# Rotated q-k scores on one core: blocks transposed in place, three input tiles each, q loads a step earlier, rotations in pairs

## Chip, cores, metric

One core of one Trainium2 chip (trn2). The metric is the device time of one execution in microseconds. The profiled span is about 1.7 us shorter than the same execution's time.

## The reference

```python
# batch 16, seq 512, heads 16, dim 64; q, k: [16, 512, 16, 64] fp32; cos, sin: [512, 32]
q_rot = concat([q1 * cos - q2 * sin, q1 * sin + q2 * cos])   # q1, q2: halves of dim
k_rot = the same of k
scores = einsum('bshd,bthd->bsht', q_rot, k_rot)             # [16, 512, 16, 512] fp32
```

67.24 MB come in, 268.44 MB go out.

## The kernel before

A step is one quarter of a batch (128 rows of s, all 16 heads); there are 64. Row s is p*4+c, so that each partition reads and writes long runs (packets of 16 and 32 KB in the trace). VectorE rotates q and k in place in the loaded tile (two products, one sum), TensorE transposes 128x128 blocks into PSUM, VectorE or ScalarE copies them to kT or qT, TensorE forms the scores (two heads at a time, 64 rows of the array each), ScalarE copies these to one of three staging tiles, and SyncE issues the store.

```python
    in_pool = ctx.enter_context(tc.tile_pool(name="in", bufs=2))
    kt_pool = ctx.enter_context(tc.tile_pool(name="kt", bufs=2))
    qt_pool = ctx.enter_context(tc.tile_pool(name="qt", bufs=2))
    stage_pool = ctx.enter_context(tc.tile_pool(name="stage", bufs=3))
    ...
        for i in range(C, NST):                 # C = 4, NST = 64
            tr = {}
            if i + 1 < NST:
                tr[1], tr[3] = ("q", i + 1, 0), ("q", i + 1, 1)
            if i + C < NST:
                tr[5], tr[6] = ("k", i + C, 0), ("k", i + C, 1)
            dve = []
            if i + 2 < NST:
                dve += rope("q", i + 2)
            if i + 1 + C < NST:
                dve += rope("k", i + 1 + C)
            ...
            for p in range(HP):                 # 8 pairs of heads
                scores(i, p, st)
                if p not in tr:
                    continue
                if tr[p][0] == "q":
                    run(dve[:1])
                    dve = dve[1:]
                    transposed(*tr[p], nc.vector.tensor_copy)
                else:
                    transposed(*tr[p], nc.scalar.copy)
            run(dve)
            if i % C == C - 2:
                load("q", i // C + 2)
            elif i % C == C - 1:
                load("k", i // C + 3)
```

The last store is cut: all but the last two heads first, then these as a piece of 116 rows and one of 12.

Of the kernel before, what the change touches and what calls it, by code (L numbers as in the profile page):

```python
# [10 lines left out]
def kernel(  # L11
# [8 lines left out]
    nc = tc.nc  # L20
    fp32 = mybir.dt.float32
# [3 lines left out]
    B, S, H, D = q.shape  # L25
    HD = D // 2
    P = 128
    C = S // P
    HP = H // 2
    NST = B * C  # L30
    G = H // C

# [3 lines left out]
    kt_pool = ctx.enter_context(tc.tile_pool(name="kt", bufs=2))  # L36
    qt_pool = ctx.enter_context(tc.tile_pool(name="qt", bufs=2))
# [9 lines left out]
    o_v = out.rearrange("b (p c) h t -> b c p h t", c=C)  # L47
# [5 lines left out]
    ss_v = ss_t.rearrange("p c x j -> p c (x j)")  # L53



    st_first = [stage_pool.tile([P, H, S], fp32, tag="stage", name="st") for _ in range(2)]
    early = stage_pool.tile([P, 2 * C * H * D], fp32, tag="stage", name="early")
# [12 lines left out]
    batches = {}  # L71

    def load(which, b):

        if b >= B:
            return
        t = in_pool.tile([P, C, H * D], fp32, tag=which + "_in", name=which + "_sb")
        batches[which, b] = t
        nc.sync.dma_start(t.rearrange("p c (h d) -> p c h d", h=H), dram[which][b])

    def rope(which, n):


        part = part_pool.tile([P, H * D], fp32, tag="part", name="part")
        if n < C:
            x = units[which, n]
            sv, k1, k2 = "p c (g j) -> p c g j", {"j": HD}, {"j": D}
            cs = cos_t.unsqueeze(2).to_broadcast((P, C, 2 * G, HD))
            ss = ss_v.unsqueeze(2).to_broadcast((P, C, G, D))
            pv = part.rearrange("p (c g j) -> p c g j", c=C, j=D)  # L90
            x5 = x.rearrange("p c (h x j) -> p c h x j", x=2, j=HD)
            p5 = part.rearrange("p (c h x j) -> p c h x j", c=C, x=2, j=HD)
            adds = [(x5[:, :, :, y], p5[:, :, :, 1 - y]) for y in range(2)]
        else:
            x = batches[which, n // C][:, n % C]
            sv, k1, k2 = "p (g j) -> p g j", {"j": HD}, {"j": D}
            cs = cos_t[:, n % C].unsqueeze(1).to_broadcast((P, 2 * H, HD))
            ss = ss_v[:, n % C].unsqueeze(1).to_broadcast((P, H, D))
            pv = part.rearrange(sv, **k2)
            x4 = x.rearrange("p (h x j) -> p h x j", x=2, j=HD)  # L100
            swapped = bass.AP(part.tensor, part.offset + HD, [part.ap[0], (D, H), (-HD, 2), (1, HD)])
            adds = [(x4, swapped)]
        xs, xc = x.rearrange(sv, **k2), x.rearrange(sv, **k1)

        def products():
            nc.vector.tensor_tensor(pv, xs, ss, op=mult)  # L106
            nc.vector.tensor_tensor(xc, xc, cs, op=mult)  # L107

        def sums():
            for y, z in adds:  # L110
                nc.vector.tensor_tensor(y, y, z, op=add)  # L111

        return [products, sums]

    kT = {}
    qT = {}

    def transposed(which, n, g, copy):


        bank = ps_t_pool.tile([P, 4, P], fp32, tag="ps_t", name="bank")
        for x in range(4):
            if n < C:
                src = units[which, n][:, x, P * g : P * (g + 1)]
            else:
                src = batches[which, n // C][:, n % C, P * (4 * g + x) : P * (4 * g + x + 1)]
            nc.tensor.transpose(bank[:, x, :], src, ident)  # L127
        src = bank
        if which == "q":
            if n not in qT:  # L130
                qT[n] = qt_pool.tile([P, HP, P], fp32, tag="qT", name="qT_t")
            dst = qT[n][:, 4 * g : 4 * g + 4, :]
        else:
            b = n // C
            if b not in kT:
                kT[b] = kt_pool.tile([P, HP, S], fp32, tag="kT", name="kT_t")
            if n < C:
                dst = kT[b][:, 2 * n + g].rearrange("p (t c) -> p t c", c=C)
                src = bank.rearrange("p c t -> p t c")
            else:  # L140
                dst = kT[b][:, 4 * g : 4 * g + 4, P * (n % C) : P * (n % C + 1)]
        copy(out=dst, in_=src)  # L142

    def store(i, st):
        o = o_v[i // C, i % C]
        if i < NST - 1:
            nc.sync.dma_start(o, st)
            return

        h = H - 2  # L150
        nc.sync.dma_start(o[:, :h], st[:, :h])
        nc.sync.dma_start(o[:116, h:], st[:116, h:])
        nc.sync.dma_start(o[116:, h:], st[116:, h:])

    def scores(i, p, st):

        ps = ps_s_pool.tile([P, 2, S], fp32, tag="ps_s", name="ps")
        b = i // C
        if b == 0:
            c, hp = divmod(p, 2)  # L160
            lhs, rhs = qT[i][:, C * hp + c], kT[0][:, 2 * i + hp]
        else:
            lhs, rhs = qT[i][:, p], kT[b][:, p]
        for r in range(2):
            po, rh = ps[:, r, :], rhs[64 * r : 64 * r + 64, :]
            nc.tensor.matmul(  # L166
                out=po, lhsT=lhs[64 * r : 64 * r + 64, :], rhs=rh, start=True, stop=True
            )
        so, si = st[:, 2 * p : 2 * p + 2, :], ps
        if b > 0:  # L170
            so = so.rearrange("s r (t c) -> s r t c", c=C)
            si = si.rearrange("s r (c t) -> s r t c", c=C)
        nc.scalar.copy(out=so, in_=si)  # L173
        if b == 0 and p % 2 == 1:
            c = p // 2
            nc.sync.dma_start(o_v[0, c, :, G * i : G * (i + 1)], st[:, G * c : G * (c + 1)])
        elif b > 0 and p == HP - 1:
            store(i, st)
# [9 lines left out]
    with tc.manual_schedule():  # L188
# [6 lines left out]
        load("q", 1)  # L195
# [8 lines left out]
        for i in range(C):  # L204
            st = st_first[i] if i < 2 else stage_pool.tile([P, H, S], fp32, tag="stage", name="st")
# [6 lines left out]
            for p in range(HP):  # L212
                scores(i, p, st)
                if p in (0, 1) and i > 0:
                    run(dve[:1])
                    dve = dve[1:]
                    transposed("k", C + i - 1, p, nc.vector.tensor_copy)
                if p == 3 and i < 2:
                    load("kq"[i], 2)
# [9 lines left out]
        for i in range(C, NST):  # L229
            tr = {}  # L230
# [5 lines left out]
            if i + 2 < NST:  # L236
                dve += rope("q", i + 2)
            if i + 1 + C < NST:
                dve += rope("k", i + 1 + C)
            st = stage_pool.tile([P, H, S], fp32, tag="stage", name="st")  # L240
            for p in range(HP):
                scores(i, p, st)
# [9 lines left out]
            if i % C == C - 2:  # L252
                load("q", i // C + 2)
            elif i % C == C - 1:
                load("k", i // C + 3)
# [30 lines left out]
```

## Time and profile before

| | kernel before |
|---|---|
| time, median of 3 | 801.34 us (800.51 to 801.43) |
| span | 799.0 us |
| moved | 336.17 MB, 421 GB/s mean, 429 from 20 to 720 us |
| busy: TensorE, ScalarE, VectorE | 87%, 70%, 68% |

The prediction shows the page, the stages and the waits. The groups of the two operations that the change or its rivals touch (line, engine, operation, output<-input, shape, count | busy us, mean ns | idle before, and its releaser):

```profile
L173 ACT COPY st<-ps 128x1024 f32<-128x1024 f32 x512 | 494.7, 1018 | 203.7 <-DMA out_dram<-st 105.6
L166 PE MATMUL ps<-kT_t,qT_t 64*128 64x512 f32 x2048 | 548.9, 654 | 71.0 <-ACT st L173 70.9
```

The columns of the stages are stretch, length, busy of TensorE, weight loads, VectorE, ScalarE, GpSimd, granted clock, share of the 16 transfer engines, GB/s.

```profile
84.00:88.00 4.00, 4.00 (x22) 1.83 (x20) 3.73 (x5) 3.48 (x4) 0.00 (x0) 1.00 1.05 446
88.00:92.00 4.00, 4.00 (x22) 1.83 (x20) 3.91 (x4) 3.33 (x5) 0.00 (x0) 1.00 0.97 418
92.00:96.00 4.00, 4.00 (x20) 1.69 (x18) 3.30 (x4) 3.55 (x5) 0.00 (x0) 1.00 1.01 434
96.00:100.00 4.00, 4.00 (x22) 1.72 (x18) 3.29 (x4) 3.21 (x4) 0.00 (x0) 1.00 1.05 451
```

The transfers are busy throughout; VectorE too, and TensorE runs close behind it.

### The profile page before, as it was taken

The numbers are of one execution on the slowest core, as the hardware profiler recorded it, in microseconds if no ns is written. First come the engines' busy times: TensorE is split into PE (matmuls) and PEld (weight loads), VectorE is DVE, ScalarE is ACT, GpSimd is POOL, SyncE is SP. The second block draws the span as 40 slices with busy tenths as digits, with TensorE's granted clock in tenths as the row PEclk, the third lists the DMA queues.
The fourth block names the chain that finished last, engine by engine and source line by source line (L and its number), as shares of the span: only waits on it lengthen the run. The fifth ranks groups of instructions, "written<-read, shape, count | busy, mean of one in ns | idle before, by whom it ended". The sixth has DMA issues, their size and how long they took to land.

```text
span 799.0 us, 7715 instructions
## 1 busy us (share of the span) xinstructions
PE 691.3 (87%) x3072; PEld 299.3 (37%) x3072; DVE 544.6 (68%) x516; ACT 561.2 (70%) x647; POOL 0.7 (0%) x6
## 2 busy tenths in 40 slices
PE   4989998997979979799797997979979799799970
PEld 2444443343434334343343443424434343344420
DVE  6999987676866768577585775857758478585300
ACT  3888886775857758577585775757757677578870
POOL 0000000000000000000000000000000000000000
PEclk9999999898998989889898898988989899899995
DMA  9999999999999999999999999999999999998995
GB/s 355 422 424 424 432 427 433 425 435 427 421 437 426 439 427 430 433 431 430 431 428 433 434 428 429 433 438 420 418 426 434 435 415 418 426 440 375 422 439 231
DMA packets 17844, 336.17 MB, mean 421 GB/s; under 512 B 1808, under 2 KB 3088, under 8 KB 4240
## 3 DMA queue, kind: packets, MB, share of 16 engines
q1 hardware_dynamic: 17520, 335.55, 98.6%
q8 instruction: 24, 0.39, 0.2%
q10 hardware_dynamic: 288, 0.13, 0.1%
q14 instruction: 12, 0.10, 0.0%
HBM read 67.24 MB, written 268.44 MB: 420 GB/s over the span
## 4 chain that ended last, share of the span: by engine, by line
DMA 50%; PE 40%; ACT 4%; DVE 3%; issue 1%; ACTq 0%; SPq 0%; DVEq 0%
DMA out_dram<-st 47%; PE ps L166 30%; PE bank L127 10%; ACT st L173 4%; DMA q_sb<-in_q_dram 2%; DVE part L106 1%; DMA early<-in_k_dram 1%; DVE q_sb L107 0%; DVE k_sb L107 0%; DVE k_sb L111 0%; DVE q_sb L111 0%; DVE early L107 0%; DVE kT_t L142 0%; ACTq L281 0%; DVE early L111 0%
## 5 line engine op out<-in xcount | busy, mean ns | idle before, releaser
L173 ACT COPY st<-ps 128x1024 f32<-128x1024 f32 x512 | 494.7, 1018 | 203.7 <-DMA out_dram<-st 105.6
L166 PE MATMUL ps<-kT_t,qT_t 64*128 64x512 f32 x2048 | 548.9, 654 | 71.0 <-ACT st L173 70.9
L166 PEld LDWEIGHTS ps<-kT_t,qT_t 64*128 64x128 f32 x2048 | 185.0, 197 | 261.7 <-issue 144.6
L142 DVE COPY qT_t<-bank 128x512 f32<-128x512 f32 x118 | 81.6, 691 | 203.8 <-PE bank L127 203.8
L127 PEld LDWEIGHTS bank<-ident,q_sb 128*128 128x128 f32 x480 | 55.6, 152 | 102.5 <-issue 99.1
L127 PE MATMUL bank<-ident,q_sb 128*128 128x128 f32 x480 | 86.9, 308 | 0.9 <-PE ps L166 0.9
L127 PEld LDWEIGHTS bank<-ident,k_sb 128*128 128x128 f32 x480 | 50.5, 141 | 95.4 <-issue 38.7
L127 PE MATMUL bank<-ident,k_sb 128*128 128x128 f32 x480 | 78.7, 287 | 1.6 <-DVE qT_t L142 1.2
L142 ACT COPY kT_t<-bank 128x512 f32<-128x512 f32 x122 | 72.5, 599 | 6.4 <-PE bank L127 6.4
L107 DVE TENSOR_TENSOR q_sb<-q_sb,cos_t 128x1024 f32<-128x1024 f32 x60 | 73.5, 1226 | 2.1
L111 DVE TENSOR_TENSOR k_sb<-k_sb,part 128x1024 f32<-128x1024 f32 x60 | 73.5, 1225 | 2.1
L107 DVE TENSOR_TENSOR k_sb<-k_sb,cos_t 128x1024 f32<-128x1024 f32 x60 | 73.5, 1225 | 2.0
L106 DVE TENSOR_TENSOR part<-q_sb,ss_t 128x1024 f32<-128x1024 f32 x60 | 73.5, 1225 | 2.0
L106 DVE TENSOR_TENSOR part<-k_sb,ss_t 128x1024 f32<-128x1024 f32 x60 | 73.0, 1216 | 0.1
L111 DVE TENSOR_TENSOR q_sb<-q_sb,part 128x1024 f32<-128x1024 f32 x60 | 73.0, 1216 | 0.0
L127 PE MATMUL bank<-ident,early 128*128 128x128 f32 x64 | 10.5, 316 | 12.5 <-DVE early L111 10.6
L127 PEld LDWEIGHTS bank<-ident,early 128*128 128x128 f32 x64 | 8.3, 161 | 17.5 <-issue 13.4
L106 DVE TENSOR_TENSOR part<-early,ss_t 128x1024 f32<-128x1024 f32 x8 | 9.8, 1223 | 5.9 <-DMA early<-in_k_dram 5.8
L111 DVE TENSOR_TENSOR early<-early,part 128x512 f32<-128x512 f32 x16 | 10.3, 687 | 0.2
L107 DVE TENSOR_TENSOR early<-early,cos_t 128x1024 f32<-128x1024 f32 x8 | 9.8, 1225 | 0.3
L142 ACT COPY qT_t<-bank 128x512 f32<-128x512 f32 x10 | 5.7, 617 | 3.2 <-PE bank L127 3.2
L142 DVE COPY kT_t<-bank 128x512 f32<-128x512 f32 x6 | 4.1, 685 | 0.3 <-PE bank L127 0.3
(9 smaller groups left out, 2.8 us busy)
## 6 DMA issues: line engine op xcount, KB each, us to landing
out_dram<-st SPq DMA_DIRECT2D x59, 4096.0 KB, 23.9
k_sb<-in_k_dram SPq DMA_DIRECT2D x15, 2048.0 KB, 26.9
q_sb<-in_q_dram SPq DMA_DIRECT2D x15, 2048.0 KB, 29.9
out_dram<-st SPq DMA_DIRECT2D x16, 1024.0 KB, 14.3
out_dram<-st SPq DMA_DIRECT2D x1, 3584.0 KB, 20.4
early<-in_k_dram SPq DMA_DIRECT2D x1, 1536.0 KB, 8.9
early<-in_q_dram SPq DMA_DIRECT2D x1, 1536.0 KB, 12.1
early<-in_k_dram SPq DMA_DIRECT2D x1, 512.0 KB
```

Of the source, the lines that this page charges most:

```text
L106: nc.vector.tensor_tensor(pv, xs, ss, op=mult)
L107: nc.vector.tensor_tensor(xc, xc, cs, op=mult)
L111: nc.vector.tensor_tensor(y, y, z, op=add)
L127: nc.tensor.transpose(bank[:, x, :], src, ident)
L142: copy(out=dst, in_=src)
L166: nc.tensor.matmul(out=po, lhsT=lhs[64 * r : 64 * r + 64, :], rhs=rh, start=True, stop=True)
L173: nc.scalar.copy(out=so, in_=si)
```

## The change

The intent: save the memory of kT and qT and give it to a third input tile each for q and k, spread the loads over the steps, and let one VectorE instruction do two slots (2.28 to 2.29 us in the run, against 2 x 1.22 for single ones).

```diff
-    kt_pool = ctx.enter_context(tc.tile_pool(name="kt", bufs=2))
-    qt_pool = ctx.enter_context(tc.tile_pool(name="qt", bufs=2))
+    BUFS = {"k": 3, "q": 3}
 ... rope(which, n, count): the same three instructions over `count` slots; scratch of 2 * H * D
 def transposed(which, n, g, copy):
-        copy(out=dst, in_=src)                 # dst in kT or qT
+        copy(out=x, in_=bank)                  # back to where the block was read
 def scores(lhs, rhs, so):
-                out=po, lhsT=lhs[64 * r : 64 * r + 64, :], rhs=rh, start=True, stop=True
+                out=ps[:, r, :].rearrange("s (c t) -> s c t", c=C),
+                lhsT=lhs[64 * r : 64 * r + 64],
+                rhs=rhs[64 * r : 64 * r + 64],     # four runs of 128, 4 KB apart
 ... in the steps:
-            if i + 2 < NST:
-                dve += rope("q", i + 2)
-            if i + 1 + C < NST:
-                dve += rope("k", i + 1 + C)
+            if i % 2 == 0 and i + 2 < NST:
+                dve += rope("q", i + 2, 2)
+            if i == C:
+                dve += rope("k", 2 * C + 1)
+            if i % 2 == 1 and i + 1 + C < NST:
+                dve += rope("k", i + 1 + C, 2)
-            if i % C == C - 2:
-                load("q", i // C + 2)
+            if c == 1:
+                load("q", b + 2)
```

The scores of the first batch now also permute in ScalarE's copy.

More of the change, by code (lines that the diff above doesn't have):

```diff
@@ L31 @@
     G = H // C
+    QS = C
     const_pool = ctx.enter_context(tc.tile_pool(name="const", bufs=1))
@@ L46 @@
     }
-    o_v = out.rearrange("b (p c) h t -> b c p h t", c=C)
+    o_v = out.rearrange("b (p c) h t -> b p c h t", c=C)
     ident = const_pool.tile([P, P], fp32, name="ident")
@@ L53, with last, new_stage, stage @@
     ss_v = ss_t.rearrange("p c x j -> p c (x j)")
-    st_first = [stage_pool.tile([P, H, S], fp32, tag="stage", name="st") for _ in range(2)]
-    early = stage_pool.tile([P, 2 * C * H * D], fp32, tag="stage", name="early")
+    def last(o, st):
+        h = H - 2
+        nc.sync.dma_start(o[:, :h], st[:, :h])
+        nc.sync.dma_start(o[:116, h:], st[:116, h:])
+        nc.sync.dma_start(o[116:, h:], st[116:, h:])
+    def new_stage():
+        return stage_pool.tile([P, H, S], fp32, tag="stage", name="st")
+    st_first = [new_stage(), new_stage()]
+    early = new_stage().rearrange("p h t -> p (h t)")
+    def stage(i):
+        return st_first[i] if i < 2 else new_stage()
+    def store(i, st):
+        b, c = divmod(i, C)
+        if i == NST - 1:
+            last(o_v[b, :, c], st)
+        else:
+            nc.sync.dma_start(o_v[b, :, c], st)
     units = {}
@@ L69, in load_units, with load, rope @@
             units[which, (head + h) // G] = t[:, :, D * h : D * (h + G)]
-    batches = {}
-    def load(which, b):
+    tiles = {}
+    SLOTS = {"k": C, "q": QS}
+    BUFS = {"k": 3, "q": 3}
+    def load(which, m):
+        n = SLOTS[which]
+        b, c = divmod(m * n, C)
         if b >= B:
             return
-        t = in_pool.tile([P, C, H * D], fp32, tag=which + "_in", name=which + "_sb")
-        batches[which, b] = t
-        nc.sync.dma_start(t.rearrange("p c (h d) -> p c h d", h=H), dram[which][b])
-    def rope(which, n):
-        part = part_pool.tile([P, H * D], fp32, tag="part", name="part")
+        t = in_pool.tile(
+            [P, n, H * D], fp32, tag=which + "_in", bufs=BUFS[which], name=which + "_sb"
+        )
+        for x in range(n):
+            tiles[which, m * n + x] = t, x
+        nc.sync.dma_start(
+            t.rearrange("p c (h d) -> p c h d", h=H), dram[which][b, :, c : c + n]
+        )
+    def rope(which, n, count=1):
+        part = part_pool.tile([P, 2 * H * D], fp32, tag="part", name="part")
         if n < C:
             x = units[which, n]
-            sv, k1, k2 = "p c (g j) -> p c g j", {"j": HD}, {"j": D}
+            part = part[:, : H * D]
             cs = cos_t.unsqueeze(2).to_broadcast((P, C, 2 * G, HD))
             ss = ss_v.unsqueeze(2).to_broadcast((P, C, G, D))
-            pv = part.rearrange("p (c g j) -> p c g j", c=C, j=D)
             x5 = x.rearrange("p c (h x j) -> p c h x j", x=2, j=HD)
@@ L93, in rope @@
             adds = [(x5[:, :, :, y], p5[:, :, :, 1 - y]) for y in range(2)]
+            nc_ = C
         else:
-            x = batches[which, n // C][:, n % C]
-            sv, k1, k2 = "p (g j) -> p g j", {"j": HD}, {"j": D}
-            cs = cos_t[:, n % C].unsqueeze(1).to_broadcast((P, 2 * H, HD))
-            ss = ss_v[:, n % C].unsqueeze(1).to_broadcast((P, H, D))
-            pv = part.rearrange(sv, **k2)
-            x4 = x.rearrange("p (h x j) -> p h x j", x=2, j=HD)
-            swapped = bass.AP(part.tensor, part.offset + HD, [part.ap[0], (D, H), (-HD, 2), (1, HD)])
+            t, y = tiles[which, n]
+            x = t[:, y : y + count]
+            part = part[:, : count * H * D]
+            c = n % C
+            cs = cos_t[:, c : c + count].unsqueeze(2).to_broadcast((P, count, 2 * H, HD))
+            ss = ss_v[:, c : c + count].unsqueeze(2).to_broadcast((P, count, H, D))
+            x4 = x.rearrange("p c (h x j) -> p (c h) x j", x=2, j=HD)
+            swapped = bass.AP(
+                part.tensor, part.offset + HD, [part.ap[0], (D, count * H), (-HD, 2), (1, HD)]
+            )
             adds = [(x4, swapped)]
-        xs, xc = x.rearrange(sv, **k2), x.rearrange(sv, **k1)
+            nc_ = count
+        pv = part.rearrange("p (c g j) -> p c g j", c=nc_, j=D)
+        xs = x.rearrange("p c (g j) -> p c g j", j=D)
+        xc = x.rearrange("p c (g j) -> p c g j", j=HD)
         def products():
@@ L113, in rope, with block, q_block @@
         return [products, sums]
-    kT = {}
-    qT = {}
+    def block(which, n, hp):
+        if n == 0:
+            return units[which, hp // 2][:, :, P * (hp % 2) : P * (hp % 2 + 1)]
+        return tiles[which, C * n][0][:, :, P * hp : P * (hp + 1)]
+    def q_block(n, c, hp):
+        if n == 0:
+            return block("q", 0, hp)[:, c]
+        t, y = tiles["q", C * n + c]
+        return t[:, y, P * hp : P * (hp + 1)]
     def transposed(which, n, g, copy):
         bank = ps_t_pool.tile([P, 4, P], fp32, tag="ps_t", name="bank")
-        for x in range(4):
-            if n < C:
-                src = units[which, n][:, x, P * g : P * (g + 1)]
-            else:
-                src = batches[which, n // C][:, n % C, P * (4 * g + x) : P * (4 * g + x + 1)]
-            nc.tensor.transpose(bank[:, x, :], src, ident)
-        src = bank
-        if which == "q":
-            if n not in qT:
-                qT[n] = qt_pool.tile([P, HP, P], fp32, tag="qT", name="qT_t")
-            dst = qT[n][:, 4 * g : 4 * g + 4, :]
-        else:
-            b = n // C
-            if b not in kT:
-                kT[b] = kt_pool.tile([P, HP, S], fp32, tag="kT", name="kT_t")
-            if n < C:
-                dst = kT[b][:, 2 * n + g].rearrange("p (t c) -> p t c", c=C)
-                src = bank.rearrange("p c t -> p t c")
-            else:
-                dst = kT[b][:, 4 * g : 4 * g + 4, P * (n % C) : P * (n % C + 1)]
-        copy(out=dst, in_=src)
@@ L144, in store @@
-    def store(i, st):
-        o = o_v[i // C, i % C]
-        if i < NST - 1:
-            nc.sync.dma_start(o, st)
-            return
-        h = H - 2
-        nc.sync.dma_start(o[:, :h], st[:, :h])
-        nc.sync.dma_start(o[:116, h:], st[:116, h:])
-        nc.sync.dma_start(o[116:, h:], st[116:, h:])
-    def scores(i, p, st):
-        ps = ps_s_pool.tile([P, 2, S], fp32, tag="ps_s", name="ps")
-        b = i // C
-        if b == 0:
-            c, hp = divmod(p, 2)
-            lhs, rhs = qT[i][:, C * hp + c], kT[0][:, 2 * i + hp]
-        else:
-            lhs, rhs = qT[i][:, p], kT[b][:, p]
+        if n < C:
+            x = block(which, 0, 2 * n + g)
+        else:
+            t, y = tiles[which, n]
+            x = t[:, y, 4 * P * g : 4 * P * (g + 1)].rearrange("p (g e) -> p g e", e=P)
@@ L164, in scores @@
+        for y in range(4):
+            nc.tensor.transpose(bank[:, y, :], x[:, y], ident)
+        copy(out=x, in_=bank)
+    def scores(lhs, rhs, so):
+        ps = ps_s_pool.tile([P, 2, S], fp32, tag="ps_s", name="ps")
         for r in range(2):
-            po, rh = ps[:, r, :], rhs[64 * r : 64 * r + 64, :]
             nc.tensor.matmul(
-                out=po, lhsT=lhs[64 * r : 64 * r + 64, :], rhs=rh, start=True, stop=True
-            )
-        so, si = st[:, 2 * p : 2 * p + 2, :], ps
@@ L170, in scores @@
-        if b > 0:
-            so = so.rearrange("s r (t c) -> s r t c", c=C)
-            si = si.rearrange("s r (c t) -> s r t c", c=C)
-        nc.scalar.copy(out=so, in_=si)
-        if b == 0 and p % 2 == 1:
-            c = p // 2
-            nc.sync.dma_start(o_v[0, c, :, G * i : G * (i + 1)], st[:, G * c : G * (c + 1)])
-        elif b > 0 and p == HP - 1:
-            store(i, st)
+                out=ps[:, r, :].rearrange("s (c t) -> s c t", c=C),
+                lhsT=lhs[64 * r : 64 * r + 64],
@@ L180, in tr_act @@
+                rhs=rhs[64 * r : 64 * r + 64],
+                start=True,
+                stop=True,
+            )
+        nc.scalar.copy(
+            out=so.rearrange("s r (t c) -> s r t c", c=C),
+            in_=ps.rearrange("s r (c t) -> s r t c", c=C),
+        )
     def tr_act(which, n):
@@ L194 @@
         load("k", 1)
-        load("q", 1)
+        load("q", C // QS)
         make_identity(nc, ident)
@@ L204 @@
         for i in range(C):
-            st = st_first[i] if i < 2 else stage_pool.tile([P, H, S], fp32, tag="stage", name="st")
+            st = stage(i)
             if i < C - 1:
@@ L212 @@
             for p in range(HP):
-                scores(i, p, st)
+                c, hp = divmod(p, 2)
+                hp += 2 * i
+                scores(q_block(0, c, hp), block("k", 0, hp), st[:, 2 * p : 2 * p + 2])
                 if p in (0, 1) and i > 0:
@@ L217 @@
                     transposed("k", C + i - 1, p, nc.vector.tensor_copy)
+                if p % 2 == 1:
+                    nc.sync.dma_start(
+                        o_v[0, :, c, G * i : G * (i + 1)], st[:, G * c : G * (c + 1)]
+                    )
                 if p == 3 and i < 2:
@@ L229 @@
         for i in range(C, NST):
+            b, c = divmod(i, C)
             tr = {}
@@ L235 @@
             dve = []
-            if i + 2 < NST:
-                dve += rope("q", i + 2)
-            if i + 1 + C < NST:
-                dve += rope("k", i + 1 + C)
-            st = stage_pool.tile([P, H, S], fp32, tag="stage", name="st")
+            if i % 2 == 0 and i + 2 < NST:
[4 more added lines that the diff above has]
+                dve += rope("k", i + 1 + C, 2)
+            st = stage(i)
             for p in range(HP):
-                scores(i, p, st)
+                scores(q_block(b, c, p), block("k", b, p), st[:, 2 * p : 2 * p + 2])
                 if p not in tr:
@@ L251 @@
             run(dve)
-            if i % C == C - 2:
-                load("q", i // C + 2)
-            elif i % C == C - 1:
-                load("k", i // C + 3)
+            store(i, st)
+            if c == 1:
+                load("q", b + 2)
+            elif c == C - 1:
+                load("k", b + 3)
 _INS = ['q', 'k', 'cos', 'sin']
```

## The prediction

> **What bounds the kernel now.** I began with the page of the kernel before: busy shares, slices, queues.
>
> ```profile
> span 799.0 us, 7715 instructions
> PE 691.3 (87%) x3072; PEld 299.3 (37%) x3072; DVE 544.6 (68%) x516; ACT 561.2 (70%) x647; POOL 0.7 (0%) x6
> ...
> DMA  9999999999999999999999999999999999998995
> GB/s 355 422 424 424 432 427 433 425 435 427 421 437 426 439 427 430 433 431 430 431 428 433 434 428 429 433 438 420 418 426 434 435 415 418 426 440 375 422 439 231
> ...
> q1 hardware_dynamic: 17520, 335.55, 98.6%
> q8 instruction: 24, 0.39, 0.2%
> ```
>
> TensorE shows 87%, but its row counts pipelined matmuls; the transfer engines are at 90% or more in all slices but the dip (slice 37) and the last. 336.17 MB is the traffic that the task itself demands: 67.24 MB of q, k, cos and sin, 268.44 MB of scores. The second view cuts the span into stages; its last two columns are the busy share of the 16 transfer engines and their GB/s.
>
> ```profile
> 20.00:720.00 700.00, 629.54 (x2809) 271.56 (x2807) 510.37 (x481) 507.49 (x587) 0.00 (x0) 0.93 1.00 429
> 720.00:740.00 20.00, 19.38 (x86) 8.56 (x88) 11.60 (x11) 16.80 (x20) 0.00 (x0) 0.91 0.90 384
> 740.00:780.00 40.00, 33.91 (x150) 13.84 (x146) 8.77 (x10) 30.45 (x33) 0.00 (x0) 0.96 0.98 421
> 780.00:790.00 10.00, 0.00 (x0) 0.00 (x0) 0.00 (x0) 0.00 (x0) 0.00 (x0) 0.62 0.93 390
> 790.00:799.00 9.00, 0.00 (x0) 0.00 (x0) 0.00 (x0) 0.00 (x0) 0.00 (x0) 0.50 0.17 65
> ```
>
> From 20 to 720 us the share is 1.00: no room. At 429 GB/s the bytes need 336.17/0.429 = 784 us, so 15 us of the span are start, dip and tail: the first 20 us at 355 GB/s lose 20 x 74/429 = 3.4 us, the dip 20 x 45/429 = 2.1 us, the last 19 us (10 at 390, 9 at 65) 0.9 + 7.6 = 8.5 us, the stretch between 0.7 us.
>
> The third view is who waited for whom.
>
> ```profile
> DVE qT_t L142 <- PE bank L127: 203.8, 113, 7.1
> ...
> ACT st L173 <- DMA out_dram<-st: 105.6, 28, 6.0
> ```
>
> ScalarE waits 28 times for a store to give back one of three staging tiles; TensorE's wait on ScalarE is the same wait handed on. VectorE is idle 203.8 us because it is early. All three compute engines have slack against the transfers: a step of 64 queues 5.25 MB (12.2 us at 429 GB/s), while the chain shows TensorE passing undisturbed steps in 10.02 us (its pieces recur at 80.08, 90.10 and 100.12).
>
> Last, I read the trace's landing records. Each transfer counts up its semaphore sixteen times. Lag from the eighth to the sixteenth: 0.7 us for a transfer landing at 25 us, 2.9 at 101, 5.3 at 298, 7.5 at 397, 10.4 at 645. For the store that ScalarE waits on at 719.56 us they are at 709.4 and 719.46. So some engine falls steadily behind and, ten microseconds late, never runs dry. In the dip the others wait and it does not: its lag drops from 10.6 to 8.7 us. The store before the last stands at 780.5 and 789.2 us, the last big one at 789.0 and 797.8. That late engine, busy from about 2 to 797.8 us, sets the end; the 7.6 us of tail are the other engines waiting for it (and for the 464 KB piece of the last store, done at about the same time).
>
> [...]
>
> **The change, part by part.**
>
> *Pairs on VectorE.* The order of the changed kernel's instructions has 168 tensor_tensor of 2048 elements in place of 336 of 1024 (56 pairs of three). [...] VectorE's idle time only grows. Worth on the path: 0.
>
> *Transposes in place.* The counts stay: 1024 scores matmuls, 512 transposes in 128 groups of four, 124 PSUM copies on VectorE (0.69 us) and the rest on ScalarE (0.60 us). The scores now read k as four runs of 128 elements, 4 KB apart, where the copy tile was one run of 512. Only a large slowdown could show: TensorE's 10.02 us a step may grow by 2 us before reaching 12.2. The copy of the first batch's scores now permutes, but all 512 copies before take 1012 to 1048 ns, permuted or not. Value 0.
>
> *Buffers.* By the code, per partition: k and q tiles from 2 x 2 x 16 to 2 x 3 x 16 KB, the rotation scratch from 4 to 8, and 32 KB of kT and 8 KB of qT go: 204 to 200 KB. The staging tiles stay at three, and it is those that ScalarE waits for.
>
> *Loads.* The 15 later q loads go out after the second step of a batch instead of the third, so k and q loads alternate every second step. Bytes, row lengths and engines are the same. The adjacent loads delayed some stores more than others, but the engines were fully busy all the while, so evening it out shifts waits and removes no transfer. Loads have time: q is issued 4 steps (49 us) and k 3 steps (37 us) before its first product, against 29.9 and 26.9 us to landing. The dip may move or vanish; that frees 2 us of the quick engines, none of the late one. Value 0, at most 2 us.
>
> *Start of the steady part.* One place gets worse. In 20 to 80 us VectorE is 97% busy and TensorE trails it (a 1.23 us wait at 69.3 us). Step 4 now gets a q pair and one k slot, 3 x 2.29 + 3 x 1.22 = 10.5 us, where it had 7.3. The products ahead of the first q copy take 4.6 instead of 2.4 us, and the sums ahead of the second 2.3 instead of 1.2: the k transposes, which need those PSUM banks back, come about 3 us later. The store of step 4 would start near 77 instead of 73.9 us. The transfers queued before it land at 78.4 us on the median engine and 81.5 on the late one, so the late one still has work. Cost: 0 to 1 us.
>
> Sum: 0 for the pairs, 0 for the transposes, 0 to -2 for the loads, 0 to +1 at the start. From 801.34 I predict **801.0 us**.
>
> **Rivals.** (a) *The loads were the trouble*: evening them out closes the dip, and the queues stay fuller. For it: the dip of 20 us at 384 GB/s, and VectorE's and ScalarE's waits. Against it: the late engine worked through the dip. It would make 797 to 799. (b) *TensorE pays for the strided operand or the in-place order*: the scores matmul groups would rise from 654 ns, and over 2 us a step the kernel would become TensorE-bound; 10% on 549 us of matmuls is 55 us of work, about 0.9 us a step, still hidden. To lose 2% a step would need 12.4 us, a quarter more than now; nothing in the trace hints at that. (c) *Longer VectorE instructions block the copies*: a q copy can stand behind 4.6 us of products. The copies' slack is VectorE's wait of 203.8 us in 113 pieces, 1.8 us each, and the products mostly run in that wait; a blocked copy costs TensorE some of its 2 us a step. It would show at steps 4 to 6 only, 802 to 804. (d) *A large gain, under 785 us*: it would need the bytes at 429 GB/s with no start or tail, 784 us. Excluded unless the late engine's lag goes.
>
> **Range and chances.** The three runs before lie within 0.9 us. A gain is limited by the late engine, whose work the change does not touch; a loss by 2 us of slack a step and a queue of up to two stores. I take 797.5 to 804.5 for 8 in 10: rival (a) at its best below, (c) at its worst above. Faster by over 2% (below 785.3) 0.01; within 2% 0.97; slower (above 817.4) 0.02.
>
> **What would show it.** Right: the stage of 20 to 720 us again at share 1.00 and 427 to 431 GB/s; the last landing lag again 8 to 11 us; [...] scores copies still waiting about 100 us for stores; matmul groups within 2% of 654 ns. Step 4 and 5 stores later by 3 to 5 us, with a share below 1 at most for 1 or 2 us near 80 us. Wrong: a share below 0.98 in the middle (then a new wait starves the queue), matmul groups above 700 ns (b), or a last lag of only a few microseconds (then the engines' load is not fixed by the bytes as I hold, and the gain could pass my range).

The sum came to 801.0 us: 801.34 with 0 for the pairs, 0 for the transposes, 0 to -2 for the loads and 0 to +1 at the start. The 0 for the pairs stands on VectorE's wait of 203.8 us. The 2.29 us of a pair, on which the term for the start rests, no trace had shown yet; the changed kernel's shows it: 2.28 to 2.29 us, 4.6 us of products ahead of the first q copy, 10.5 us for the six instructions of step 4. That matmuls overlap is read from the groups (2048 records of 654 ns would be 1339 us; TensorE is busy with them for 549). The sixteen counts of a transfer are those of 112 transfers in the trace; the two pieces of the last store count 4 and 12.

## The result

801.63 us (801.17 to 802.38, 6 runs) against 800.63 (800.03 to 801.43, 6 runs) for the kernel before: ratio 1.0011, 95% interval 0.9998 to 1.0024. Same within 2%: about one microsecond slower, two at most by the interval, and no difference at all is not excluded. (A ratio is the mean time of one kernel's runs over the mean of the other's of the same rounds, so it is not quite the ratio of the medians.)

The page after; compare the span, VectorE's busy time and the slices with the prediction's first fence:

```profile
span 800.1 us, 7591 instructions
PE 689.7 (86%) x3072; PEld 298.5 (37%) x3072; DVE 515.9 (64%) x348; ACT 561.3 (70%) x647; POOL 0.7 (0%) x6
...
GB/s 353 416 427 431 381 412 431 430 428 428 431 434 425 430 422 431 434 428 432 430 428 437 429 433 427 436 430 434 430 422 419 430 431 437 424 419 424 425 435 223
```

VectorE lost 28.7 us of work and 168 instructions, and the time did not fall. The dip of slice 37 (375) is gone, and a new one stands in slice 5 (381). The stages, in the prediction's cuts:

```profile
20.00:720.00 700.00, 629.19 (x2799) 271.09 (x2797) 486.30 (x320) 507.22 (x586) 0.00 (x0) 0.93 1.00 427
720.00:740.00 20.00, 20.00 (x98) 8.85 (x96) 9.36 (x7) 17.38 (x20) 0.00 (x0) 1.00 0.99 422
740.00:780.00 40.00, 31.89 (x146) 12.98 (x144) 6.26 (x7) 29.98 (x32) 0.00 (x0) 0.98 1.00 430
```

The long stage is full as before (1.00). The groups and the largest waits are those of before:

```profile
L187 ACT COPY st<-ps 128x1024 f32<-128x1024 f32 x512 | 495.1, 1019 | 204.1 <-DMA out_dram<-st 110.9
L180 PE MATMUL ps<-k_sb,q_sb 64*128 64x512 f32 x1920 | 512.1, 650 | 69.8 <-ACT st L187 69.8
```

ScalarE waits for stores 110.9 us (105.6 before), and a scores matmul takes 650 ns (654), four runs 4 KB apart or not. The new dip is near the start:

```profile
84.00:88.00 4.00, 2.92 (x16) 1.30 (x14) 3.97 (x4) 2.31 (x4) 0.00 (x0) 1.00 0.87 373
88.00:92.00 4.00, 4.00 (x22) 1.70 (x18) 4.00 (x3) 3.48 (x5) 0.00 (x0) 1.00 0.93 393
92.00:96.00 4.00, 4.00 (x21) 1.68 (x20) 3.97 (x4) 3.33 (x5) 0.00 (x0) 1.00 0.91 393
96.00:100.00 4.00, 4.00 (x22) 1.96 (x22) 2.32 (x2) 3.85 (x5) 0.00 (x0) 1.00 0.93 303
```

For 16 us the transfers run at 0.87 to 0.93. The time line of step 4 shows how it comes about; first the kernel before (start, length, engine, line, operation), then the changed one:

```profile
68.58 0.68 DVE L142 COPY qT_t<-bank 128x512 f32<-128x512 f32 x1
70.31 0.68 DVE L142 COPY qT_t<-bank 128x512 f32<-128x512 f32 x1
71.05 0.66 PE L127 MATMUL bank<-ident,k_sb 128*128 128x128 f32 x4
73.85 0.33 SPq L147 DMA_DIRECT2D out_dram<-st  x1
```

```profile
68.28 2.29 DVE L142 TENSOR_TENSOR q_sb<-q_sb,cos_t 128x2048 f32<-128x2048 f32 x1
70.49 0.68 DVE L173 COPY q_sb<-bank 128x512 f32<-128x512 f32 x1
71.09 2.28 DVE L146 TENSOR_TENSOR q_sb<-q_sb,part 128x2048 f32<-128x2048 f32 x1
73.29 0.69 DVE L173 COPY q_sb<-bank 128x512 f32<-128x512 f32 x1
74.03 0.66 PE L172 MATMUL bank<-ident,k_sb 128*128 128x128 f32 x4 [0.72 <-DVE q_sb L173]
76.83 0.33 SPq L75 DMA_DIRECT2D out_dram<-st  x1
```

The pair's products and sums stand ahead of the two q copies, which come 1.9 and 3.0 us later. The k transposes wait for the PSUM bank that the second copy frees, and the store of step 4 goes out at 76.83 instead of 73.85 us. Step 5 adds to it: its store goes out at 88.54 instead of 83.86 us.

The landing records of the trace (112 transfers count up a semaphore sixteen times each; eighth and sixteenth count, us from the start of the span; not a view of the page, so printed as a table):

```
                              before            changed
a store near 100 us        97.91  100.84     100.29  100.68
a store near 300 us       293.04  298.36     295.88  300.69
store before the last     780.47  789.24     779.96  790.28
last large piece          789.03  797.80     788.55  798.88
```

One engine is late in both kernels: the last large piece has its fifteenth count at 790.87 us before and at 792.43 in the changed kernel, and its sixteenth 6.9 and 6.4 us later. In the changed one its lag is down to 0.4 us near 100 us: there it too had run dry. Once the same bytes have landed (the stores of steps 4 to 6 and one q load), the sixteenth count stands at 116.42 us against 115.39 before, 1.0 us later. From there the lag grows again, to 10.3 us, and the last landing is 1.1 us later than before.

### The profile page after: what moved, and what is told of

It reads as the page before. It is cut to its first block, busy times and chain, and to the rows that moved or that the text cites. A ratio compares the mean times of both kernels' runs of the same rounds, so it can differ in the third digit from the quotient of the medians. Undisturbed runs are those within 1.5% of the kernel's fastest.

```text
span 800.1 us, 7591 instructions
## 1 busy us (share of the span) xinstructions
PE 689.7 (86%) x3072; PEld 298.5 (37%) x3072; DVE 515.9 (64%) x348; ACT 561.3 (70%) x647; POOL 0.7 (0%) x6
## 3 DMA queue, kind: packets, MB, share of 16 engines
q1 hardware_dynamic: 17520, 335.55, 98.5%
## 4 chain that ended last, share of the span: by engine, by line
DMA 45%; PE 39%; DVE 8%; ACT 5%; issue 1%; ACTq 0%
DMA out_dram<-st 45%; PE ps L180 29%; PE bank L172 10%; ACT st L187 4%; DVE part L141 2%; DVE k_sb L142 1%; DVE k_sb L146 1%; DVE st L146 1%; DVE st L142 1%; DVE q_sb L142 1%; DVE q_sb L146 1%; DVE k_sb L173 0%; DVE q_sb L173 0%; ACTq L304 0%; ACT st L173 0%
## 5 line engine op out<-in xcount | busy, mean ns | idle before, releaser
L187 ACT COPY st<-ps 128x1024 f32<-128x1024 f32 x512 | 495.1, 1019 | 204.1 <-DMA out_dram<-st 110.9
L180 PE MATMUL ps<-k_sb,q_sb 64*128 64x512 f32 x1920 | 512.1, 650 | 69.8 <-ACT st L187 69.8
L180 PEld LDWEIGHTS ps<-k_sb,q_sb 64*128 64x128 f32 x1920 | 172.3, 196 | 246.2 <-issue 129.8
L173 DVE COPY q_sb<-bank 128x512 f32<-128x512 f32 x118 | 81.4, 690 | 235.6 <-PE bank L172 235.6
L141 DVE TENSOR_TENSOR part<-k_sb,ss_t 128x2048 f32<-128x2048 f32 (+1 forms) x33 | 69.0, 2091 | 3.1 <-DMA k_sb<-in_k_dram 2.9
L142 DVE TENSOR_TENSOR k_sb<-k_sb,cos_t 128x2048 f32<-128x2048 f32 (+1 forms) x33 | 69.2, 2098 | 2.0
L142 DVE TENSOR_TENSOR q_sb<-q_sb,cos_t 128x2048 f32<-128x2048 f32 (+1 forms) x31 | 68.9, 2223 | 1.1
L146 DVE TENSOR_TENSOR k_sb<-k_sb,part 128x2048 f32<-128x2048 f32 (+1 forms) x33 | 69.0, 2090 | 0.2
L141 DVE TENSOR_TENSOR part<-q_sb,ss_t 128x2048 f32<-128x2048 f32 (+1 forms) x31 | 68.6, 2214 | 0.1
L173 ACT COPY k_sb<-bank 128x512 f32<-128x512 f32 x114 | 67.9, 596 | 1.1 <-PE bank L172 1.1
L146 DVE TENSOR_TENSOR q_sb<-q_sb,part 128x2048 f32<-128x2048 f32 (+1 forms) x31 | 68.6, 2213 | 0.0
L172 PE MATMUL bank<-ident,st 128*128 128x128 f32 x64 | 10.5, 316 | 12.3 <-DVE st L146 10.4
L146 DVE TENSOR_TENSOR st<-st,part 128x512 f32<-128x512 f32 x16 | 10.3, 687 | 0.2
(12 smaller groups left out, 17.8 us busy)
## 6 DMA issues: line engine op xcount, KB each, us to landing
st<-in_q_dram SPq DMA_DIRECT2D x1, 1536.0 KB, 12.2
```

The costliest lines, as they stand in the source:

```text
L141: nc.vector.tensor_tensor(pv, xs, ss, op=mult)
L142: nc.vector.tensor_tensor(xc, xc, cs, op=mult)
L146: nc.vector.tensor_tensor(y, y, z, op=add)
L172: nc.tensor.transpose(bank[:, y, :], x[:, y], ident)
L173: copy(out=x, in_=bank)
L180: nc.tensor.matmul(out=ps[:, r, :].rearrange("s (c t) -> s c t", c=C), lhsT=lhs[64 * r : 64 * r + 64], rhs=rhs[64 * r : 64 * r + 64], star ...
```

## The experiments

Theory: one of the sixteen transfer engines has more to do than the others, is busy almost from start to end, and sets the time; VectorE's, TensorE's and ScalarE's times have slack, except where they let this engine run dry. Rivals: the loads' spacing, the VectorE work, or the strided operand each have an effect, and they cancel; or the tail is just the last store's small piece. Each ratio below is against the kernel before on the same chip in the same rounds, with five rounds (four to six executions of each).

| run | median us | ratio | 95% interval |
|---|---|---|---|
| changed kernel | 801.63 | 1.0011 | 0.9998 to 1.0024 |
| in_place_only | 801.33 | 1.0005 | 0.9993 to 1.0018 |
| one_slot (in place, early loads) | 800.08 | 0.9990 | 0.9978 to 1.0003 |
| loads_back (in place, pairs) | 803.05 | 1.0026 | 1.0014 to 1.0039 |
| pairs_later | 799.75 | 0.9987 | 0.9974 to 1.0001 |
| later_loads_back | 800.59 | 0.9991 | 0.9977 to 1.0005 |
| last_even | 802.78 | 1.0029 | 1.0016 to 1.0042 |
| spare15 | 820.33 | 1.0209 | 1.0164 to 1.0254 |
| spare12to15 | 814.57 | 1.0169 | 1.0138 to 1.0200 |
| spare_small | 806.55 | 1.0064 | 1.0051 to 1.0076 |
| pe_more | 903.13 | 1.1271 | 1.1251 to 1.1291 |
| one_pass | 796.46 | 0.9939 | 0.9927 to 0.9952 |
| one_pass_more | 804.14 | 1.0046 | 1.0032 to 1.0060 |

All gave a result that the comparison with the reference accepted.

**The q loads a step later again.**

```diff
-            if c == 1:
+            if c == 2:
                 load("q", b + 2)
```

> The changed kernel with its q loads after the third step of a batch again, as before. Theory (one late transfer engine sets the end; waits before stores are only moved about): no difference from the changed kernel, 801.6 us, ratio to the kernel before 1.000 to 1.002, last landing lag again 9 to 11 us; the share of the transfers may dip near 728 us again. Rival (spacing the loads gained 1 to 3 us and something else in the change took it back): 803 to 805 us.

Measured 803.05 us: my "no difference" was wrong by 1.4 us, the last lag was 7.9 us and not 9 to 11, and the rival's range (803 to 805) holds the time. The dry stretch is now deeper:

```profile
84.00:88.00 4.00, 2.92 (x17) 1.28 (x17) 4.00 (x3) 2.48 (x4) 0.00 (x0) 1.00 0.96 410
88.00:92.00 4.00, 4.00 (x22) 1.68 (x18) 3.96 (x4) 3.28 (x4) 0.00 (x0) 1.00 0.67 283
92.00:96.00 4.00, 4.00 (x22) 1.83 (x20) 4.00 (x3) 3.42 (x5) 0.00 (x0) 1.00 0.91 393
96.00:100.00 4.00, 4.00 (x22) 1.68 (x19) 2.80 (x2) 3.76 (x5) 0.00 (x0) 1.00 0.92 393
```

0.67 from 88 to 92 us instead of 0.93: without the q load issued after step 5 there is less to move while the late stores are awaited. The dip near 728 us also came back (share 0.84 from 720 to 740 us). Neither is where the late engine lost the 1.4 us, as a table below shows.

**One slot at a time on VectorE.**

```diff
-            if i % 2 == 0 and i + 2 < NST:
-                dve += rope("q", i + 2, 2)
-            ...
+            if i + 2 < NST:
+                dve += rope("q", i + 2)
+            if i + 1 + C < NST:
+                dve += rope("k", i + 1 + C)
```

> The changed kernel with every slot rotated on its own, as before; buffers, in-place transposes and loads stay changed. Theory: VectorE's busy time goes back from 516 to about 543 us and the kernel does not get slower for it; since the overload of step 4 goes too, the dry stretch at 84 to 96 us goes (share 1.00 there) and the time falls by about 1 us to 800.6. Rival (the 26 us of VectorE work saved are worth something, and another part hides it): 803 us or more.

Measured 800.08 us, ratio 0.9990; the share is 0.96 to 1.08 from 84 to 96 us. Giving VectorE its work back made the kernel no slower; the interval lies just under that of the changed kernel's 1.0011 and overlaps it.

**Pairs only from step 8 on.**

```diff
-            if i % 2 == 0 and i + 2 < NST:
+            if i < 2 * C:
+                dve += rope("q", i + 2) + rope("k", i + 1 + C)
+            elif i % 2 == 0 and i + 2 < NST:
                 dve += rope("q", i + 2, 2)
-            if i == C:
-                dve += rope("k", 2 * C + 1)
+            if i == 2 * C:
+                dve += rope("k", 3 * C + 1)
```

> The changed kernel with pairs only from step 8 on, so that the one overloaded step (a q pair and a k slot) falls where VectorE has idle time. Theory: no dry stretch at 84 to 96 us, lag at 100 us 2 to 3 us instead of 0.4, time about 1 us under the changed kernel, 800.6; VectorE about 518 us. Rival (the dry stretch cost the late engine nothing): unchanged at 801.6.

Measured 799.75 us, and the stretch is full but for its last 4 us:

```profile
84.00:88.00 4.00, 4.00 (x22) 1.88 (x20) 3.31 (x4) 3.35 (x5) 0.00 (x0) 1.00 0.97 414
88.00:92.00 4.00, 4.00 (x22) 1.68 (x20) 3.28 (x4) 3.41 (x4) 0.00 (x0) 1.00 0.99 426
92.00:96.00 4.00, 4.00 (x20) 1.64 (x20) 3.90 (x4) 3.76 (x6) 0.00 (x0) 1.00 1.07 451
96.00:100.00 4.00, 4.00 (x22) 1.93 (x22) 2.67 (x4) 3.44 (x4) 0.00 (x0) 1.00 0.90 377
```

TensorE runs 16.00 of 16 us there instead of 14.92, and the lag near 100 us is 2.3 us instead of 0.4. Pairs cost nothing measurable where VectorE has idle time (0.9987 against 0.9990 with single slots).

**The last piece over all rows.**

```diff
-        nc.sync.dma_start(o[:116, h:], st[:116, h:])
-        nc.sync.dma_start(o[116:, h:], st[116:, h:])
+        nc.sync.dma_start(o[:, h:], st[:, h:])
```

> The changed kernel, but the last 512 KB of the last store go out as one piece of 128 rows instead of pieces of 116 and 12 rows. Theory: the late engine now gets 8 rows of 4 KB more at the very end (8 x 0.16 us): 1.3 us slower, 802.9 us, although the transfer is spread over more engines; the tail stays 7 us long. Rival (the tail is the 116-row piece itself, running on few engines, and no engine is late): 3 to 6 us faster, 796 to 798 us.

Measured 802.78 us, the 802.9 that the theory gave. Spreading the last half megabyte over more engines (the pieces of 116 and 12 rows ran on four and twelve, by their landing counts) did not help; the rival (the tail is that piece itself) falls. The trace's packet records show why the odd cut of both kernels suits the late engine: after its last 28 KB packet it has a single one of 4 KB (0.16 us), a row of the 12-row piece; in last_even it has eight.

**Sparing an engine by rows.** Three tries to take work from the late engine:

```diff
+        elif i == 40:                          # spare15; spare12to15 cuts at 108
+            nc.sync.dma_start(o_v[b, :120, c], st[:120])
+            nc.sync.dma_start(o_v[b, 120:, c], st[120:])
```

> The changed kernel with the store of step 40 cut into a piece of 120 rows and one of 8 rows, and the last piece of the last store over all 128 rows. [...] Theory, if the late engine is the sixteenth: its lag jumps from 6 us to about -4 at step 40 and is under 2 us at the end; the next latest engine (4 us behind) then ends the kernel: 794 to 797 us. If the late engine is another: no gain, 802 to 804 us. Rival (no engine is late for good; the landing lag is only how a transfer ends): no gain either, and the lag curve does not jump.

> The same, but cut at 108 rows: [...] Theory, if the late engine is any of the last four: lag at the end about 0, 793 to 797 us. [...] Rival (no late engine): 3 us slower than the even last piece alone, about 806 us.

```diff
+        elif i % 8 == 4:                       # spare_small, on top of pairs_later
+            h = H - 2
+            nc.sync.dma_start(o_v[b, :, c, :h], st[:, :h])
+            nc.sync.dma_start(o_v[b, :120, c, h:], st[:120, h:])
+            nc.sync.dma_start(o_v[b, 120:, c, h:], st[120:, h:])
```

> Pairs from step 8 on, even last piece; in the store of every eighth step (seven stores from step 4 to 60 less the first batch) the last two heads go out as a piece of 120 rows and one of 8[...]; all else keeps its 128 rows. [...] Theory, if the late engine is the sixteenth: final lag 0 to 3 us, 794 to 797 us. If it is not: no gain, 801 us plus. Rival (splitting a store by rows costs in itself, as the 120-row store did): 805 us or more.

All three lost: 820.33, 814.57 and 806.55 us. In spare15 the slices after step 40 fall to 337 GB/s and stay uneven to the end, and the lag rises from 7 to 12 or 13 us instead of falling. (The six runs of spare15 lie between 812.6 and 823.7 us; whether it is slower by 2% stays unclear.) So cutting stores by rows cost time in itself here. The rival of spare_small (a cost of the cut) was right; why a cut store runs so badly stays open. By the ratios against last_even, the one cut store of 64 cost 14 us in spare15 and 11 in spare12to15. By the landing counts the pieces of 120 and 8 rows ran on 15 and 8 engines, those of 108 and 20 rows on 12 and 10 (queue q1 has 7 and 6 packets more than the 17520 of the changed kernel, one for each count more). Which engines these were is not shown: in the expectations "the sixteenth" and "the last four" are the assumption of the ones left out. The late engine took one row of the 12-row piece of the last store, but none of the 29 rows that each of four engines took of the 116-row piece. Whether either cut spared it is not known, so these three runs say nothing of what makes it late.

**More TensorE instructions.** Each group of four transposes gets four one-column dummy matmuls ahead of it.

```diff
+        for y in range(4):
+            nc.tensor.matmul(
+                out=bank[:, y, :1], lhsT=ident, rhs=ident[:, :1], start=True, stop=True
+            )
```

> The changed kernel with four tiny dummy matmuls (one column) ahead of each group of four transposes, into the bank that the transposes then overwrite: a third more TensorE instructions, about 8 more instruction packets of 16 KB, some 1 us more TensorE time a step (below its 2 us of slack). Theory (the late engine is late because it also fetches TensorE's instructions): the last lag grows from 10.3 to about 13.5 us and the time by 3 to 4 us, to 805. Rival (it is late for another reason, and compute time has slack): lag 10 us and 801.6 us unchanged.

```profile
PE 872.4 (97%) x5120; PEld 517.5 (57%) x5120; DVE 518.7 (58%) x348; ACT 571.8 (63%) x647; POOL 0.7 (0%) x6
...
q8 instruction: 40, 0.66, 0.3%
```

The run missed its purpose. A dummy took four matmul records of 254 ns each (2048 records for 512 dummies) instead of the 0.15 us that I had put down, an estimate that no trace had shown, so TensorE became the bound (97%; the chain of waits is 96% TensorE) and the queue ran dry again and again (slices of 372 to 408 GB/s in the middle), which keeps the lag under 3 us. It does show two things: the packets of q8 count TensorE's instructions (24 for 6144 records, 40 for 10240: one for 256), and TensorE's slack is exceeded when a step takes it 14 us (903/64), as the transfers need 12.2.

**In place alone.** Single slots and late q loads together (both edits above).

> In-place transposes and the three tiles alone: the changed kernel with single slots on VectorE and with q loads after the third step, both as before. Theory: the same time as the kernel before and as single slots with early loads (800.1 us): 799.5 to 801.5 us; scores matmul groups about 650 ns; share 1.00 at 84 to 104 us. Rival (reading k in runs 4 KB apart, or the in-place order, costs something that the early loads paid for): 802 to 804 us.

Measured 801.33 us, ratio 1.0005 (0.9993 to 1.0018): transposing in place and reading k in four runs cost nothing that these runs can tell.

**Pairs from step 8, loads late.**

> Pairs from step 8 on, with q loads after the third step again. The early q load was seen to be worth 1.4 us in the changed kernel. Theory now: only because it filled the dry stretch at 88 to 100 us; where that stretch is gone, it is worth nothing: 799.1 to 800.6 us, as with early loads (799.75). Rival (even spacing is worth 1.4 us by itself, through the whole run): 801 to 802 us.

Measured 800.59 us, ratio 0.9991 against 0.9987 with early loads: 0.3 us, not to be told from nothing. That fits the theory, but single slots do not: they have no dry stretch either (share 0.95 to 1.07 from 84 to 100 us in in_place_only), and the same step gave 0.9990 against 1.0005, 1.2 us, as much as with pairs (1.0011 against 1.0026), with intervals that overlap. The traces tell more. When did the late engine have the same bytes behind it? (Sixteenth count of a batch's last k load, us, in one trace of each run:)

```
stores landed                       4       16       28       48
single slots, late loads       130.94   279.22   427.75   675.40   in_place_only
single slots, early loads      130.76   279.11   426.73   673.93   one_slot
pairs, late loads              133.18   281.66   430.12   677.55   loads_back
pairs, early loads             132.96   281.21   429.00   675.88   changed kernel
```

Pairs cost 2.2 us before the first column and nothing after it: that is the dry stretch. Early loads gain 0.2 us there and then little by little, 1.5 to 1.7 us by the last column; so the gain is not made in the dry stretch. Nor is it made in the dip: across it, the late engine's counts are 9.96 to 9.98 us apart in all four. Why early loads help slowly is not shown. The first rival is thus right in part: pairs lose 1.7 us by the ratios, early loads gain 1.2 us, and the two nearly cancel.

**Fewer TensorE instructions, the same data moved.** On top of pairs_later:

```diff
-                lhsT=lhs[64 * r : 64 * r + 64],
-                rhs=rhs[64 * r : 64 * r + 64],
+                lhsT=lhs[64 * r : 64 * r + 64].bitcast(bf16)[:, 1::2],
+                rhs=rhs[64 * r : 64 * r + 64].bitcast(bf16)[:, :, 1::2],
```

> Wrong on purpose: the scores matmuls read the upper halves of the fp32 words as bf16, so each runs as one weight load and one matmul instead of two and two (4096 TensorE instructions instead of 6144; 16 instead of 24 packets of 16 KB of instructions), with pairs from step 8 on. Transfers of data are unchanged. Theory (the late engine is late because it fetches TensorE's instructions): final lag falls by a third, from 7.5 to about 5 us, time 2 to 4 us under 799.75, 796 to 798. Rival (late for another reason, and TensorE's time is off the path): lag and time as with pairs from step 8 on.

```profile
PE 448.3 (56%) x2048; PEld 214.5 (27%) x2048; DVE 519.3 (65%) x360; ACT 542.3 (68%) x647; POOL 0.7 (0%) x6
...
q8 instruction: 16, 0.26, 0.1%
```

The matmul records fell from 3072 to 2048: one for each of the 1024 scores matmuls instead of two. 796.46 us, as the theory had it: 0.48% below pairs_later by the ratios, 3.8 us for eight packets less. But the last lag was 8.7 us, not 5, and TensorE had lost 240 us of work as well. So a second run put instructions back without the time:

```diff
+        for r in (0, 1, 0, 1):
+            nc.tensor.matmul(                  # 32 columns, then overwritten
+                out=ps[:, r, :32],
+                lhsT=lhs[64 * r : 64 * r + 64].bitcast(bf16)[:, 1::2],
+                rhs=rhs[64 * r : 64 * r + 64, 0].bitcast(bf16)[:, 1:64:2],
+                start=True, stop=True,
+            )
```

> Wrong on purpose like the one-pass kernel (796.5 us, 16 instruction packets on the queue q8), with four small dummy matmuls (32 columns, one pass) ahead of each pair of scores matmuls, into columns that the real ones then overwrite: 8192 TensorE instructions, so 32 instruction packets, more than the 24 of the kernel before; TensorE busy 600 to 700 us, not above the 690 of the kernel before. Theory (instruction packets use up the late engine's time, about 0.4 us each by the 3.3 us that eight fewer gave): 796.5 + 16 x 0.4 = 803 us, 801 to 805, last lag 10 us or more. Rival (the one-pass kernel gained because TensorE was done sooner, or by its calmer clock, or because transfers never ran short of stores): not above the 799.75 us of the same kernel with full passes.

```profile
PE 466.1 (58%) x4096; PEld 242.1 (30%) x4096; DVE 519.6 (65%) x360; ACT 542.0 (68%) x647; POOL 0.7 (0%) x6
...
q8 instruction: 32, 0.52, 0.2%
```

804.14 us, inside the theory's 801 to 805, with TensorE busy 466 us (600 to 700 had been expected), 224 less than in the kernel before. TensorE's time and clock (0.722, near the 0.708 of one_pass) do not explain a kernel that is slower than both others. What grew is the number of TensorE's instructions: by the ratios (0.9939 to 1.0046) 8.6 us for 4096 more. Near 725 us the sixteenth landing count is behind the eighth by 8.6 us in one_pass, 9.7 in pairs_later and 14.1 in one_pass_more, while the fifteenth is behind by 5.3, 3.3 and 5.4. So the dose shows that the late engine's load grows with TensorE's instructions.

It does not show that the packets of q8 are that load, and the trace's packet records (again not a view of the page) speak against it. They do not name the engine, but a packet starts 3 or 4 ns before the end of the one before it on its engine, so an engine can be followed back from the landing of a transfer. A packet of q8 takes 0.88 to 1.01 us in the steady part, and the next 32 KB packet of its engine 1.58 to 1.63 us instead of 1.21: 1.3 us in all. If one engine had all 24, it would fall 31 us behind, and no lag exceeds 15. Where the late engine could be followed (1550 us in ten runs), 50 packets of q8 were moved, none by it. What sets it apart is its data. Of the 32 KB packets from 150 to 700 us, one in 15 to 20 takes 1216 to 1300 ns, and most of the late engine's are of this kind: followed back from sixteenth counts between 300 and 700 us, 150 of 208 in the kernel before and 108 of 176 in the changed one, against 0 and 7 of 256 from eighth counts (in the other kernels with 24 packets of q8 the long ones take 1240 to 1247 ns):

```
                                       one_pass  pairs_later  one_pass_more
TensorE instructions                       4096         6144           8192
packets of q8                                16           24             32
32 KB packets, median, ns                  1213         1213           1213
the long ones, mean, ns                    1238         1241           1255
lag near 725 us                             8.6          9.7           14.1
estimate                                    9.1          9.9           15.2
```

The estimate: the excess over 1213 ns on 53 stores of 8 packets (10.4, 11.8 and 17.8 us), less what the packets of q8 cost the other engines by then (15, 22 and 30 x 1.3 us, over 15 engines: 1.3, 1.9 and 2.6). It comes near the lags, also where they do not follow the dose evenly. Why this engine's packets are long, and how TensorE's instructions lengthen them, stays open; every run here was traced, so whether tracing has a part in it is not shown.

## Why the prediction was right, point by point

*What bounds.* Right. The long stage stayed at share 1.00, the last lag at 10.3 us, ScalarE's waits for stores at about 110 us. The prediction left open why an engine is late. last_even, one_pass and one_pass_more show that its load counts, and that it grows with TensorE's instructions; what lengthens its packets is still open.

*Pairs, value 0.* Right in value: pairs take 2.28 to 2.29 us, VectorE fell from 544.6 to 515.9 us, the kernel gained nothing from the work saved. (What the pairs cost at the start is a heading of its own, below.)

*Transposes in place, value 0.* Right: 650 ns against 654, and 1.0005 alone.

*Loads, 0 to -2.* Right in size, 1.2 us by the ratios, if the gain is real: the intervals overlap. It was not made in the dip of 728 us, where the prediction looked for it and saw nothing to gain for the late engine, but slowly over the whole run, which the prediction had no reason for.

*Start of the steady part, 0 to +1.* The mechanism was right to the tenth: store of step 4 at 76.83 us, "near 77"; steps 4 and 5 late by 3.0 and 4.7 us, as its signs said (3 to 5). The size was not. Only the delay of step 4 was worked through to the transfers, where "the late one still has work", and a share below 1 was expected for a microsecond or two; with step 5 the stretch lasted 16 us at about 0.91, and the late engine ran dry too. By loads_back against in_place_only this term is 0.21%, 1.7 us, more than the 1 us allowed. The early loads took back 1.2 us of it; that two misjudged terms nearly cancel, and the sum held to 0.6 us, was luck.

*Rivals.* (a) fell as it stood: the dip closed and the time did not; but the early loads do seem to gain about 1 us. (b) fell. (c) came true in its place, at steps 4 and 5, at less than its worst.

## What to carry to other kernels

Here, with the transfers at share 1.00, 28.7 us of work taken from VectorE were worth nothing, while two stores delayed by 3.0 and 4.7 us cost 1.7 us; so shift work (here the first pair) only where the engine has idle time. Look past the mean share of the sixteen engines to when the last of them lands: here the slowest one set the end (eighth and sixteenth count of the last large piece at 788.55 and 798.88 us of a span of 800.1), and its load grew with TensorE's instructions (8.6 us for 4096 more). A dose that works does not name its path: the packets of q8, the obvious one, were on other engines. None of the fair variants beat the kernel before clearly: pairs_later came to 0.9987 (0.9974 to 1.0001). one_pass did, at 0.9939, but with inputs cut to bf16, which the comparison tolerated and which is another computation.
